# A macaron layer in split fp32: the first two Strassen products of the three output projections change places, and the loads and stores around the middle one move

## The chip, the cores and the metric

The kernel runs on one core of one Trainium2 chip. The metric is the device time of one execution in microseconds (us). Before the change it is 2028.34 us, the median of three runs (2026.97 to 2028.96).

## The reference, cut to what matters

One layer over 1024 tokens of width 1024, all in float32:

```python
h = x + 0.5 * swiglu(rms_norm(h, ffn1_norm), ffn1_w_gate, ffn1_w_up, ffn1_w_down)
z = rms_norm(h, mix_norm) @ w_in             # q, k, v of two attentions, and gates ga, gb
ya = neighbourhood_attention_2d(qa, ka, va, na_rpb)
yb = windowed_gqa_sink(rope(qb), rope(kb), vb, sink_logit)
merged = sigmoid(ga) * (ya @ w_branch_a) + sigmoid(gb) * (yb @ w_branch_b)
h = h + merged @ w_out
h = h + 0.5 * swiglu(rms_norm(h, ffn2_norm), ffn2_w_gate, ffn2_w_up, ffn2_w_down)
return rms_norm(h, final_norm)
```

The hidden width of both feed-forward parts (FFN) is 2816. `swiglu(x, g, u, d)` is `(silu(x @ g) * (x @ u)) @ d`.

## The kernel before

**Split products.** Every float32 operand is split into a high and a low part (`split`, line 87): ScalarE casts the operand to the high part (L88), VectorE or GpSimd subtracts it from the operand and so makes the low part (L89). One product of two blocks is then three matmuls (`mm3`, line 137: L140, L142 and L144) into one PSUM bank.

**Strassen products.** The large products are done with seven block products, P1 to P7, instead of eight. The class `Down` (line 401) runs the second product of each stage, and is used three times: for the down projection of FFN1, for `merged @ w_out` (called the merge here) and for the down projection of FFN2. The left operand has `n` row blocks per half: 11 in the FFNs, 4 in the merge. An entry `(k, p)` is row block `p` of product `k`; it takes 4 column slices `j`, 3 matmuls each, so 12 matmuls of 128x512. The list `ORDER` says in which order the products run: before, P1, P2, P5, P6, P3, P7, P4.

**PSUM banks.** P1, P6, P7 and P4 accumulate in four banks called `g`, P2, P5 and P3 in four banks called `d`. P1, P2 and P5 start new sums, so each needs banks that are free; P6 goes on with P1's sum, P3 with P5's, P7 with P6's and P4 with P7's. After the last entry of P1, P2 and each later product, four VectorE instructions (`evict`, L499) add the sum to the result rows. P5 takes the same four `d` banks as P2, so its first matmul waits until P2's evictions are done. The stage ahead of a `Down` also leaves sums in `g` and `d` banks.

**Preparation.** `prep` (line 448) loads the left operand of an entry from DRAM where there is one (`hid` in the FFNs, `left_d` in the merge, L445), replaces a block of the weights by a difference of two blocks (L458 and L460 on VectorE, L461 and L463 on GpSimd) and splits both operands. It runs `RING` entries ahead of the matmuls (7 in the FFNs, 6 in the merge). `at_end` loads and prepares the first entries of a `Down` while the last products of the hidden stage still run.

**The merge.** Eight chunks of `merged` are computed ahead of it: 24 matmuls each with a weight block of `w_branch_a` (`branch_a`, line 858; loaded in `branch_w`, L839, split with the subtraction on GpSimd), into two banks, `g` and `d` in turn; then VectorE multiplies the two banks by the sigmoid of a gate (L1102, gate loaded at L1073) and adds (L1103). After every second chunk `combine` (line 1080) makes four left operands on GpSimd (L1086) and stores each to `left_d` in DRAM (L1087) from SyncE's queue. The eight loads of `w_out` (L436) stand in the code ahead of the chunk loop.

**What sets the order.** The kernel is written in a tile language. Its scheduler puts the instructions of each engine in an order of its own choosing that keeps the data dependences, from the order in which the code names them. ScalarE, VectorE, GpSimd and SyncE each then run their list in turn; an instruction that waits holds up all that stand behind it on its engine. SyncE's list also issues most DMAs (queue SP in the trace); GpSimd's issues the stores of the hidden stage.

Of the kernel before, what the change touches and what calls it, by code (L numbers as in the profile page):

```python
# [10 lines left out]
F32 = mybir.dt.float32  # L11
# [4 lines left out]
P = 128  # L16
T = 1024
D = 1024
NC8 = D // P
# [12 lines left out]
def f32v(ap):  # L32
    return ap.bitcast(F32)
# [3 lines left out]
def trunk_kernel(ctx, tc, x, n1, wg1, wu1, wd1, nm, win, rpb, sink, wa, wb, wo,  # L37
                 n2, wg2, wu2, wd2, nf, c_rope, c_mask_a, c_mask_b, out):
    nc = tc.nc
# [10 lines left out]
    def nm_(s):  # L50
        uid[0] += 1
        return f"{s}_{uid[0]}"
# [8 lines left out]
    fa = main.tile([P, 4096], F32, name="fa")  # L61
# [6 lines left out]
    def new_ar(g, dt=F32R):  # L68
        ar[g] = main.tile([P, 4, 1024], dt, tag=f"ar{g}", bufs=1, name=nm_("ar"))
        return ar[g]  # L70

    def slot(k):
        return ar[k // 4][:, k % 4, :]

    def bank(tag):
        return ps.tile([P, 512], F32, tag=tag, name=nm_(tag))

    def raw4():
        return main.tile([P, 1024], F32, tag="raw", bufs=4, name=nm_("raw"))

    def xs4():
        return main.tile([P, 1024], F32, tag="xs", bufs=2, name=nm_("xs"))

    def ws4():
        return main.tile([P, 1024], F32R, tag="ws", bufs=8, name=nm_("ws"))

    def split(dst_hi, dst_lo, src, eng=None):
        nc.scalar.copy(dst_hi, src)  # L88
        (eng or nc.vector).tensor_tensor(dst_lo, src, f32v(dst_hi), op=ALU.subtract)  # L89
# [9 lines left out]
    def w_cols(w, c0, n=P):  # L99
        return w[:, c0:c0 + n].rearrange("(c p) f -> p c f", p=P)  # L100
# [45 lines left out]
    def drain(gen, n=1 << 30):  # L146

        for _ in range(n):
            if next(gen, gen) is gen:
                return  # L150

    def res(t):

        return fx[t] if t < 4 else fa[:, (t - 4) * 1024:(t - 3) * 1024]
# [26 lines left out]
    B11, B21, T2, T1, B22, T3, T4 = range(7)  # L181
# [46 lines left out]
    NP = NF // 2  # L228
    PRODUCTS = ("P1", "P2", "P5", "P6", "P7", "P3", "P4")
    RIGHT = dict(P1=B11, P2=B21, P6=T2, P5=T1, P7=T3, P3=B22, P4=T4)  # L230

    def products(src, n, after, at_end, extra, ring, scaled=lambda i, m, half: False):


# [88 lines left out]
        def run():  # L323
            for q in range(len(seq)):
                prep_until(q + 1 if q < 4 else q + 8)
                yield from multiply(q)
                after(*seq[q], bks[seq[q][0]], snap[seq[q][0]], sn)
                at_end(len(seq) - 1 - q)
# [3 lines left out]
    def behind(prods):  # L332
# [9 lines left out]
        return post  # L342

    def hidden(wg, wu, at_end):

        def put(i, p, src):
# [54 lines left out]
    class Down:  # L401

        ORDER = ("P1", "P2", "P5", "P6", "P3", "P7", "P4")

        def __init__(self, n, w, scale, place, left=None, dram=None, loads={}, ring=(22, 24, 26), shift=0):
            self.n, self.w, self.scale, self.place, self.left, self.dram, self.loads = n, w, scale, place, left, dram, loads
            self.seq = [(k, p) for k in self.ORDER for p in range(n)]
            self.dk = [k for k in self.ORDER if k in dram]  # L410
            self.nd = (n + 1) // 2
# [63 lines left out]
        def at_end(self, n):  # L475

            if n == 10:
                self.load_blocks("B11")
            elif n == 7:
                self.load_left(2)  # L480
            elif n in (6, 4, 2, 0):
                if n == 2:
                    self.load_blocks("B21")
                self.prep_until(4 - n // 2)

        def multiply(self, e, j):
# [54 lines left out]

    def down_ffn(wd, src):

        place = {n: [divmod(h0 + p, 8) for p in range(NP)] for n, h0 in (("B11", 0), ("B22", NP), ("B12", NP + 7), ("B21", 2 * NP + 7))}
        place["B22"][7:] = [(f"xs{k // 2}", k % 2) for k in range(4)]
        loads = {}
        for t in range(NTT):
            loads.setdefault(2 + t, []).append(lambda d, t=t: nc.sync.dma_start(res(t), src[t * P:(t + 1) * P, :]))
        for name, e0 in (("B12", 8), ("B22", 19)):
            for a in range((NP + 1) // 2):  # L550
                loads.setdefault(e0 + a, []).append(lambda d, name=name: d.load_blocks(name, 2))
        return Down(NP, wd, 0.5, place, dram={k: hid[i] for i, k in enumerate(PRODUCTS)}, loads=loads)
# [5 lines left out]
    for g in range(7):  # L558
        new_ar(g)
    down = down_ffn(wd1[0], x2)  # L560
    hg = hidden(wg1[0], wu1[0], down.at_end)

# [270 lines left out]
            nc.scalar.copy(gt[:, n * 512:(n + 1) * 512], bs[n])  # L833
        nc.gpsimd.dma_start(g_d[dc * P:(dc + 1) * P, :], gt)

    def branch_w(w, dc, eng=None):

        r, t = raw4()[:, :512], ws4()
        nc.sync.dma_start(r.rearrange("p (c f) -> p c f", f=P), w_cols(w, dc * P))  # L839
        split(t[:, :512], t[:, 512:], r, eng)  # L840
        return [t[:, k:k + 512].rearrange("p (c f) -> p c f", f=P) for k in (0, 512)]

    Y_A, Y_B = ((12, 13), (14, 15), (20, 21), (10, 11)), ((4, 5), (6, 7), (0, 1), (2, 3))

    def branch_mm(bs, w, y):

        for c in range(4):
            mm3(bs, c == 0, c == 3, (w[0][:, c, :], w[1][:, c, :]),
                [[slot(k)[:, n * 512:(n + 1) * 512] for k in y[c]] for n in range(2)])
            yield  # L850
# [2 lines left out]
        load_pair([slot(k) for k in slots], y_d[r0:r0 + P, :], eng)  # L853

    a_order = [dc for p in range(4) for dc in (p, p + 4)]
    a_mm = []

    def branch_a(i):

        w = branch_w(wa[0], a_order[i], nc.gpsimd)  # L860
        bs = [bank("gd"[i % 2]) for _ in range(2)]
        a_mm.append((bs, branch_mm(bs, w, Y_A)))

    def merged(dc):
        return slot((16, 17, 18, 19, 24, 25, 26, 27)[dc])
# [155 lines left out]
    for n in range(1 << 30):  # L1021
# [14 lines left out]
        if n in (59, 60, 61):  # L1036
            c = (59, 60, 61).index(n)
# [7 lines left out]
    drain(fill)  # L1045


    split(slot(10), slot(11), fa[:, 3072:4096])
    for t in range(4):
        new_fx(t)  # L1050

    def load_h(t):
        nc.sync.dma_start(res(t), h_d[t * P:(t + 1) * P, :])


    left_d = dram.tile([4, 4, P, 512], F32, name="left_d")

    def quarter(k, p):
        m = merged(p + (4 if k in ("P2", "P4") else 0))
        return m[:, :512] if k in ("P1", "P2") else m[:, 512:]  # L1060

    place = dict(B11=[(0, p) for p in range(4)], B21=[(0, 4 + p) for p in range(4)],
                 B12=[(1, p) for p in range(4)], B22=[(1, 4 + p) for p in range(4)])
    loads = {t: [lambda d, t=t: load_h(t)] for t in range(NTT)}
    loads[0].append(lambda d: d.load_left(2))
    down = Down(4, wo[0], 1.0, place, quarter, {k: left_d[i] for i, k in enumerate(("P5", "P6", "P3", "P7"))},
                loads, (22, 20), 2)
    for name in ("B11", "B21", "B12", "B22"):
        down.load_blocks(name)

    def a_prep(dc):
        r, rb = raw4(), xs4()
        nc.sync.dma_start(r, g_d[dc * P:(dc + 1) * P, :])  # L1073
        nc.sync.dma_start(rb, g_d[D + dc * P:D + (dc + 1) * P, :])
        nc.scalar.activation(r, r, AF.Sigmoid)
        nc.scalar.activation(rb, rb, AF.Sigmoid)
        nc.vector.tensor_tensor(merged(dc), merged(dc), rb, op=ALU.mult)
        return r

    def combine(p):  # L1080
        a11, a12, a22 = [quarter(k, p) for k in ("P1", "P2", "P4")]
        a21 = merged(p)[:, 512:]
        s = [res(4 + 2 * (p % 2) + k // 2)[:, k % 2 * 512:k % 2 * 512 + 512] for k in range(4)]
        for i, (a, b, op) in enumerate(((a21, a22, ALU.add), (s[0], a11, ALU.subtract), (a12, s[1], ALU.subtract),
                                        (a11, a21, ALU.subtract))):
            nc.gpsimd.tensor_tensor(s[i], a, b, op=op)  # L1086
            nc.sync.dma_start(left_d[i, p], s[i])  # L1087

    nxt = a_prep(a_order[0])
    for i, dc in enumerate(a_order):  # L1090
        r = nxt
        if i + 1 < NC8:
            nxt = a_prep(a_order[i + 1])
        if i + 2 < NC8:
            branch_a(i + 2)
        if i + 1 == NC8:
            down.prep_until(2)
        bs, mm = a_mm[i]
        drain(mm)
        for n in range(2):  # L1100
            sl = slice(n * 512, (n + 1) * 512)
            nc.vector.tensor_tensor(r[:, sl], bs[n], r[:, sl], op=ALU.mult)  # L1102
        nc.vector.tensor_tensor(merged(dc), merged(dc), r, op=ALU.add)  # L1103
        if i % 2:
            combine(i // 2)


    gain = load_gain(n2[0])
    merge = down
    down = down_ffn(wd2[0], h_d)  # L1110
    hg = hidden(wg2[0], wu2[0], down.at_end)

# [75 lines left out]
```

## Time and profile before

| what | value |
|---|---|
| median of three runs | 2028.34 us |
| the profiled execution's own time | 2031.71 us |
| its span, first to last instruction | 2029.9 us |
| TensorE busy | 1952.6 us, 96% |
| VectorE busy | 1437.1 us, 71% |
| ScalarE busy | 963.4 us, 47% |
| GpSimd busy | 414.2 us, 20% |
| mean granted TensorE clock | 0.985 |

The busy share is over the whole span; a stage can differ. The granted clock is 1.00 at TensorE's full speed and 0.50 at half of it. The names in the rows are those of the program: `d<-ws,ws` is an instruction that reads two tiles called ws and writes one called d.

### The profile page before, as it was taken

The page shows a single profiled execution, that of the slowest core. Times are in us where ns is not written, and L with a number is a line of the kernel's source. Part 1 is how long each engine was busy: PE and PEld are TensorE (multiplying, and loading weights), DVE is VectorE, ACT ScalarE, POOL GpSimd, SP SyncE. Part 2 cuts the span into 40 slices and gives each one's busy share as a digit, 9 for nine tenths or more (in the row PEclk, how much of TensorE's full clock was granted, in tenths as well). Part 3 has the DMA queues.
Part 4 walks back from the last instruction along what each step waited for, and adds up shares of the span by engine and source line. Part 5 has one row for each costly group of instructions (what it writes and reads, how often), then busy time and mean ns, then how long its engine had stood idle before and what let it go on. Part 6 is the DMA issues. An engine that isn't in the chain of part 4 may idle for free. (4 is left out here: it accounts for less than half of the span.)

```text
span 2029.9 us, 25701 instructions
## 1 busy us (share of the span) xinstructions
PE 1952.6 (96%) x8968; PEld 1619.9 (80%) x8968; DVE 1437.1 (71%) x2479; ACT 963.4 (47%) x1857; POOL 414.2 (20%) x410
## 2 busy tenths in 40 slices
PE   6999999999999899999999999798999999999998
PEld 5788888888788788788877878586888888887886
DVE  7866566568857777478888855989756656678664
ACT  7433333344346533378887862255333333343453
POOL 4110010004301632111222124404100100114100
PEclk9999999999999999999999999899999999999999
DMA  6423323376234377452334456434332332393341
GB/s 199 135 91 107 115 90 107 114 263 232 90 95 133 120 221 199 135 151 76 104 111 125 163 177 233 151 103 143 118 116 92 104 116 93 117 348 127 103 135 63
DMA packets 224226, 279.83 MB, mean 138 GB/s; under 512 B 13376, under 2 KB 154048, under 8 KB 224096
## 3 DMA queue, kind: packets, MB, share of 16 engines
q1 hardware_dynamic: 204704, 213.58, 33.6%
q0 software_dynamic: 19392, 64.60, 8.9%
q8 instruction: 71, 1.16, 0.2%
q14 instruction: 59, 0.48, 0.1%
HBM read 195.72 MB, written 82.50 MB: 137 GB/s over the span
## 5 line engine op out<-in xcount | busy, mean ns | idle before, releaser
L140 PE MATMUL g<-ar,ws 128*128 128x512 f32 x1208 | 456.2, 399 | 9.6 <-ACT ar L88 4.4
L142 PE MATMUL g<-ar,ws 128*128 128x512 f32 x1208 | 449.1, 393 | 3.7 <-DVE ar L89 3.7
L144 PE MATMUL g<-ar,ws 128*128 128x512 f32 x1208 | 448.3, 393 | 1.8 <-DVE ws L89 1.3
L89 DVE TENSOR_TENSOR ws<-raw,ws 128x512 fp32r<-128x512 f32 (+1 forms) x335 | 254.4, 762 | 202.7 <-ACT ws L88 201.4
L88 ACT CAST ws<-raw 128x512 fp32r<-128x512 f32 (+1 forms) x343 | 217.3, 638 | 318.7 <-PE d L144 124.8
L142 PEld LDWEIGHTS g<-ar,ws 128*128 128x128 f32 x1208 | 228.9, 190 | 52.6 <-DVE ar L89 4.5
L144 PEld LDWEIGHTS g<-ar,ws 128*128 128x128 f32 x1208 | 228.6, 189 | 51.4 <-DVE ws L89 2.1
L140 PEld LDWEIGHTS g<-ar,ws 128*128 128x128 f32 x1208 | 223.4, 190 | 52.3 <-ACT ar L88 6.0
L140 PE MATMUL d<-ar,ws 128*128 128x512 f32 x656 | 255.1, 393 | 7.0 <-DVE ar L89 7.0
L142 PE MATMUL d<-ar,ws 128*128 128x512 f32 x656 | 254.8, 392 | 0.2 <-POOL ar L89 0.2
L144 PE MATMUL d<-ar,ws 128*128 128x512 f32 x656 | 254.4, 392 | 0.1
L347 POOL DMA_DIRECT2D hid<-fx x98 | 52.9, 540 | 498.8 <-DVE fx L374 374.6
L140 PEld LDWEIGHTS d<-ar,ws 128*128 128x128 f32 x656 | 124.4, 190 | 33.7 <-ACT ar L88 4.6
L142 PEld LDWEIGHTS d<-ar,ws 128*128 128x128 f32 x656 | 124.4, 190 | 26.5 <-POOL ar L89 0.6
L144 PEld LDWEIGHTS d<-ar,ws 128*128 128x128 f32 x656 | 124.3, 190 | 26.5 <-POOL ws L89 0.5
L89 DVE TENSOR_TENSOR ws<-ar,ws 128x512 fp32r<-128x512 f32 x110 | 103.7, 948 | 9.1 <-ACT ws L88 7.1
L88 ACT CAST ar<-raw 128x512 fp32r<-128x512 f32 (+1 forms) x83 | 56.0, 678 | 100.0 <-PE g L142 41.4
L89 DVE TENSOR_TENSOR ws<-fa,ws 128x512 fp32r<-128x512 f32 x80 | 55.3, 692 | 63.7 <-ACT ws L88 63.3
L140 PE MATMUL g<-ws,ws 128*128 128x512 f32 x240 | 95.1, 396 | 3.8 <-DVE raw L1102 3.2
L144 PE MATMUL g<-ws,ws 128*128 128x512 f32 x240 | 94.2, 393 | 0.0
L142 PE MATMUL g<-ws,ws 128*128 128x512 f32 x240 | 94.1, 392 | 0.0
L969 ACT ACTIVATE fa<-fa,nmx 128x385 f32<-128x385 f32 (+3 forms) x128 | 75.5, 591 | 28.6 <-DVE nmx L966 27.8
(218 smaller groups left out, 3582.9 us busy)
## 6 DMA issues: line engine op xcount, KB each, us to landing
raw<-hid SPq DMA_DIRECT2D x70, 512.0 KB
hid<-fx POOLq DMA_DIRECT2D x98, 256.0 KB, 2.6
ar<-in_ffn_w_down_dram SPq DMA_DIRECT2D x34, 512.0 KB
raw<-in_ffn_w_up_dram SPq DMA_DIRECT2D x32, 512.0 KB
raw<-in_ffn_w_gate_dram SPq DMA_DIRECT2D x28, 512.0 KB
hid<-fa POOLq DMA_DIRECT2D x56, 256.0 KB, 2.6
raw<-in_w_in_dram SPq DMA_DIRECT2D x27, 512.0 KB
z_d<-fa POOLq DMA_DIRECT2D x36, 256.0 KB, 3.4
```

Of the source, the lines that this page charges most:

```text
L88: nc.scalar.copy(dst_hi, src)
L89: (eng or nc.vector).tensor_tensor(dst_lo, src, f32v(dst_hi), op=ALU.subtract)
L140: nc.tensor.matmul(b, lhs[0], r[0], start=first, stop=False, **kw)
L142: nc.tensor.matmul(b, lhs[0], r[1], start=False, stop=False, **kw)
L144: nc.tensor.matmul(b, lhs[1], r[0], start=False, stop=last, **kw)
L347: nc.gpsimd.dma_start(hid[PRODUCTS.index(p), i], src)
L969: nc.scalar.activation(pr, pr, AF.Exp, scale=-1.0, bias=nmx[:, s:s + 1], accum_out=ssum[:, s:s + 1])
```

## The change

`ORDER` begins with P2, then P1; so P1's entries stand between the last matmul of P2 and the first of P5. To have P2's weights (B21) at hand in the FFNs, `at_end` loads B21 at its third step, ahead of the first `prep`, and `down_ffn` gives B21 and B12 each other's places. In the merge, six of the eight branch weights are loaded into a tile of their own (`fetch_branch`) before the first of `w_branch_b`; the stores of left operands are issued from GpSimd; the loads of `w_out` are named in four parts over the chunks; the gates are prepared two chunks ahead; the last block of `y` and the ring slots move to other tiles.

```diff
-        ORDER = ("P1", "P2", "P5", "P6", "P3", "P7", "P4")
+        ORDER = ("P2", "P1", "P5", "P6", "P3", "P7", "P4")
...
-            elif n in (6, 4, 2, 0):
-                if n == 2:
-                    self.load_blocks("B21")
+            elif n == 6:
+                self.load_blocks("B21")
+            elif n in (4, 2, 0):
                 self.prep_until(4 - n // 2)
...
-        place = {n: [divmod(h0 + p, 8) for p in range(NP)] for n, h0 in (("B11", 0), ("B22", NP), ("B12", NP + 7), ("B21", 2 * NP + 7))}
+        place = {n: [divmod(h0 + p, 8) for p in range(NP)] for n, h0 in (("B11", 0), ("B22", NP), ("B21", NP + 7), ("B12", 2 * NP + 7))}
...
-    def branch_w(w, dc, eng=None):
-
-        r, t = raw4()[:, :512], ws4()
+    def fetch_branch(r, w, dc):
         nc.sync.dma_start(r.rearrange("p (c f) -> p c f", f=P), w_cols(w, dc * P))
+        return r
+
+    def branch_w(w, dc, eng=None, r=None):
+
+        t = ws4()
+        if r is None:
+            r = fetch_branch(raw4()[:, :512], w, dc)
...
-        w = branch_w(wa[0], a_order[i], nc.gpsimd)
+        w = branch_w(wa[0], a_order[i], nc.gpsimd, a_raw.get(i))
...
-    split(slot(10), slot(11), fa[:, 3072:4096])
+    t = new_ar(2, F32)
+    for i in range(2, NC8):
+        a_raw[i] = fetch_branch(t[:, (i - 2) // 2, i % 2 * 512:i % 2 * 512 + 512], wa[0], a_order[i])
+    split(slot(22), slot(23), fa[:, 3072:4096])
...
-                loads, (22, 20), 2)
-    for name in ("B11", "B21", "B12", "B22"):
-        down.load_blocks(name)
+                loads, (8, 10))
...
-            nc.sync.dma_start(left_d[i, p], s[i])
-
-    nxt = a_prep(a_order[0])
+            nc.gpsimd.dma_start(left_d[i, p], s[i])
+
+    nxt = [a_prep(a_order[i]) for i in range(2)]
     for i, dc in enumerate(a_order):
-        r = nxt
-        if i + 1 < NC8:
-            nxt = a_prep(a_order[i + 1])
+        r = nxt.pop(0)
         if i + 2 < NC8:
+            nxt.append(a_prep(a_order[i + 2]))
             branch_a(i + 2)
+        if i % 2 == 0:
+            down.load_blocks(("B21", "B11", "B12", "B22")[i // 2])
+        if i + 3 == NC8:
+            new_ar(2)
```

In the built programs, these are TensorE's first matmuls of the merge's products P1, P2 and P5 (P1 and P2 have four entries of 12 matmuls each; most of them are left out), in the kernel before:

```order
L144 MATMUL d_10748<-ar_4766,ws_10743 128x512
L140 MATMUL g_10867<-ws_10819,ws_10818 128x512
...
L140 MATMUL g_10870<-ar_84 128x512
L142 MATMUL g_10870<-ar_84 128x512
L144 MATMUL g_10870<-ar_84 128x512
L140 MATMUL d_10972<-ws_10887,ws_10886 128x512
...
L140 MATMUL d_11063<-ar_84 128x512
```

and in the changed kernel:

```order
L140 MATMUL d_10864<-ws_10816,ws_10815 128x512
...
L140 MATMUL d_10867<-ws_10882,ws_10881 128x512
L142 MATMUL d_10867<-ws_10882,ws_10881 128x512
L144 MATMUL d_10867<-ws_10882,ws_10881 128x512
L140 MATMUL g_10971<-ar_10750 128x512
...
L140 MATMUL d_11060<-ws_10950,ws_10949 128x512
```

Before, P1 is in g, P2 in d and P5 in d right behind it. Now P2 stands first, in d, then P1 in g, then P5 in d. P2's first entry follows the last chunk, which is in d as well.

This is VectorE's list in the merge from behind P1's evictions to the first of P2's (L499, d) in the kernel before; fx are the result rows, the raw tiles left operands from `left_d`:

```order
L89 TENSOR_TENSOR ar_84<-raw_10872,ar_84 128x512
L89 TENSOR_TENSOR ar_84<-ar_10533,ar_84 128x512
L460 TENSOR_TENSOR ar_10533<-ar_10538,ar_10533 128x512 x2
L89 TENSOR_TENSOR ws_10998<-raw_10874,ws_10998 128x512
L89 TENSOR_TENSOR ws_10999<-ar_10533,ws_10999 128x512
L460 TENSOR_TENSOR ar_10533<-ar_10538,ar_10533 128x512
L89 TENSOR_TENSOR ws_11018<-raw_10874,ws_11018 128x512
L89 TENSOR_TENSOR ws_11019<-ar_10533,ws_11019 128x512
L460 TENSOR_TENSOR ar_10533<-ar_10538,ar_10533 128x512
L89 TENSOR_TENSOR ws_11041<-raw_10876,ws_11041 128x512
L89 TENSOR_TENSOR ws_11042<-ar_10533,ws_11042 128x512
L499 SCALAR_TENSOR_TENSOR fx_10528<-d_10972,fx_10528 128x512
```

and in the changed kernel, from the multiplication of the last chunk (L1111, L1102 before) on:

```order
L1111 TENSOR_TENSOR raw_10738<-d_10749,raw_10738 128x512
L1112 TENSOR_TENSOR ar_10212<-ar_10212,raw_10738 128x1024
L89 TENSOR_TENSOR ws_10881<-ar_10212,ws_10881 128x512
L89 TENSOR_TENSOR ws_10882<-ar_10567,ws_10882 128x512
L89 TENSOR_TENSOR ws_10908<-ar_10211,ws_10908 128x512
L89 TENSOR_TENSOR ws_10909<-ar_10567,ws_10909 128x512
L458 TENSOR_TENSOR ar_10567<-ar_10708,ar_10567 128x512
L89 TENSOR_TENSOR ws_10927<-ar_10211,ws_10927 128x512
...
L89 TENSOR_TENSOR ws_10949<-raw_10869,ws_10949 128x512
L89 TENSOR_TENSOR ws_10950<-ar_10567,ws_10950 128x512
L499 SCALAR_TENSOR_TENSOR fx_10536<-d_10864,fx_10536 128x512
```

Before, P2's evictions (d) stand behind most of P5's and P6's preparation. Now they stand right behind the preparation of P5's first entry, and P1's (g) 12 instructions after those.

This is SyncE's list in the merge before, with g_d the gates:

```order
L436 DMA ar_10533<-in_w_out_dram 128x2x512 x4
L436 DMA ar_10538<-in_w_out_dram 128x2x512 x3
L839 DMA raw_10611<-in_w_branch_a_dram 128x4x128
L1087 DMA left_d<-fa 128x512
L1073 DMA raw_10645<-g_d 128x1024
L1087 DMA left_d<-fa 128x512 x3
L839 DMA raw_10652<-in_w_branch_a_dram 128x4x128
```

and in the changed kernel:

```order
L436 DMA ar_10567<-in_w_out_dram 128x2x512 x4
L436 DMA ar_10708<-in_w_out_dram 128x2x512 x3
L1079 DMA raw_10608<-g_d 128x1024
L1079 DMA raw_10649<-g_d 128x1024
L1079 DMA raw_10696<-g_d 128x1024
L1079 DMA raw_10738<-g_d 128x1024
L445 DMA raw_10869<-left_d 128x2x512
```

The eight loads of `w_out` still stand in one piece. The branch weights and the stores to `left_d` are gone from between the gates.

## Rows read from the trace of the kernel before

**Rows 1.** the head of the page: span, then busy time of each engine

```profile
span 2029.9 us, 25701 instructions
...
PE 1952.6 (96%) x8968; PEld 1619.9 (80%) x8968; DVE 1437.1 (71%) x2479; ACT 963.4 (47%) x1857; POOL 414.2 (20%) x410
```

**Rows 2.** waits of TensorE: total us, times, longest

```profile
PE d L140 <- DVE fx L499: 16.8, 3, 12.1
...
PE g L140 <- DVE raw L1102: 3.2, 1, 3.2
...
PE g L140 <- DVE fx L362: 0.7, 1, 0.7
PE g L144 <- POOL ws L89: 0.4, 1, 0.4
```

**Rows 3.** timeline of TensorE: start, us, instruction, [idle before <-releaser]

```profile
456.35 0.39 PE L140 MATMUL g<-ws,ws 128*128 128x512 f32 x1
...
519.99 0.47 PE L140 MATMUL d<-ws,ws 128*128 128x512 f32 x1 [2.67 <-DVE fx L499]
...
1273.19 0.39 PE L140 MATMUL g<-ws,ws 128*128 128x512 f32 x1
...
1277.86 0.50 PE L140 MATMUL g<-ws,ws 128*128 128x512 f32 x1 [3.15 <-DVE raw L1102]
...
1312.27 0.77 PE L140 MATMUL d<-ar 128*128 128x512 f32 x1 [12.07 <-DVE fx L499]
...
1325.24 0.39 PE L140 MATMUL g<-ws,ws 128*128 128x512 f32 x1
...
1869.31 0.60 PE L140 MATMUL d<-ws,ws 128*128 128x512 f32 x1 [2.02 <-DVE fx L499]
```

**Rows 4.** windows: us, busy by engine, then PEclk, DMA share, GB/s

```profile
521.20:524.70 3.50, 3.50 (x10) 2.69 (x9) 2.84 (x5) 0.26 (x1) 1.12 (x1) 0.51 0.00 0
1272.80:1300.00 27.20, 24.05 (x99) 19.19 (x97) 27.20 (x27) 5.41 (x10) 15.47 (x10) 0.94 0.40 136
1278.90:1282.40 3.50, 3.50 (x10) 2.71 (x9) 3.50 (x5) 2.18 (x4) 2.19 (x2) 0.51 0.71 240
1312.20:1316.50 4.30, 4.23 (x10) 3.39 (x11) 2.92 (x5) 0.00 (x0) 0.00 (x0) 0.50 0.20 70
1869.50:1872.90 3.40, 3.40 (x9) 2.65 (x9) 3.40 (x7) 0.00 (x0) 0.00 (x1) 0.50 0.09 29
```

**Rows 5.** timeline of VectorE around the merge

```profile
1268.53 1.27 DVE L1102 TENSOR_TENSOR raw<-d,raw 128x512 f32<-128x512 f32 x2
...
1271.46 5.74 DVE L89 TENSOR_TENSOR ws<-ar,ws 128x512 fp32r<-128x512 f32 x4
...
1277.13 1.28 DVE L1102 TENSOR_TENSOR raw<-g,raw 128x512 f32<-128x512 f32 x2
...
1311.45 2.47 DVE L499 SCALAR_TENSOR_TENSOR fx<-d,fx 128x512 f32<-128x512 f32 x4
```

**Rows 6.** waits of ScalarE, 1170 to 1312 us

```profile
ACT ws L88 <- DMA raw<-in_w_branch_a_dram: 21.9, 6, 9.6
...
ACT ws L88 <- DMA raw<-left_d: 8.5, 1, 8.5
```

**Rows 7.** windows at the start of FFN1's down projection

```profile
428.00:464.00 36.00, 35.34 (x156) 28.93 (x155) 23.16 (x39) 15.68 (x28) 3.78 (x7) 1.00 1.00 362
468.00:484.00 16.00, 16.00 (x72) 13.27 (x71) 10.98 (x12) 6.86 (x12) 7.29 (x5) 1.00 1.00 373
484.00:517.50 33.50, 33.32 (x148) 27.25 (x146) 33.33 (x38) 13.87 (x25) 18.46 (x12) 1.00 0.37 104
```

**Rows 8.** timeline of VectorE in the same stretch

```profile
453.06 0.68 DVE L369 TENSOR_TENSOR fa<-d,fa 128x512 f32<-128x512 f32 x1
...
481.29 0.69 DVE L458 TENSOR_TENSOR ar<-ar,ar 128x512 f32<-128x512 f32 x1 [4.98 <-DMA ar<-in_ffn_w_down_dram]
```

**Rows 9.** DMA issues on the page: KB each, median us to landing

```profile
hid<-fx POOLq DMA_DIRECT2D x98, 256.0 KB, 2.6
```

More of the change, by code (lines that the diff above doesn't have):

```diff
@@ L834, in gate @@
         nc.gpsimd.dma_start(g_d[dc * P:(dc + 1) * P, :], gt)
-    def branch_w(w, dc, eng=None):
-        r, t = raw4()[:, :512], ws4()
+    def fetch_branch(r, w, dc):
         nc.sync.dma_start(r.rearrange("p (c f) -> p c f", f=P), w_cols(w, dc * P))
+        return r
[3 more added lines that the diff above has]
+            r = fetch_branch(raw4()[:, :512], w, dc)
         split(t[:, :512], t[:, 512:], r, eng)
         return [t[:, k:k + 512].rearrange("p (c f) -> p c f", f=P) for k in (0, 512)]
-    Y_A, Y_B = ((12, 13), (14, 15), (20, 21), (10, 11)), ((4, 5), (6, 7), (0, 1), (2, 3))
+    Y_A, Y_B = ((12, 13), (14, 15), (20, 21), (22, 23)), ((4, 5), (6, 7), (0, 1), (2, 3))
     def branch_mm(bs, w, y):
@@ L855, in trunk_kernel @@
     a_order = [dc for p in range(4) for dc in (p, p + 4)]
-    a_mm = []
+    a_mm, a_raw = [], {}
     def branch_a(i):
-        w = branch_w(wa[0], a_order[i], nc.gpsimd)
+        w = branch_w(wa[0], a_order[i], nc.gpsimd, a_raw.get(i))
         bs = [bank("gd"[i % 2]) for _ in range(2)]
```

## The prediction

> **What bounds the kernel now.** I read the head of the page first: TensorE is busy 1952.6 of 2029.9 us [rows 1], so about 77 us of the span are without a matmul, and only those, and what a low clock costs beside them, can be won. Next I read TensorE's waits by releaser [rows 2]: the largest group is `d L140 <- DVE fx L499`, 16.8 us in three waits, a matmul that starts in a d bank and waits for an eviction. TensorE's timeline puts the three at the start of P5: 2.67 us at 519.99 (FFN1), 12.07 us at 1312.27 (merge), 2.02 us at 1869.31 (FFN2) [rows 3]. That is the wait which `ORDER` decides: P5 takes the banks that P2 has just left. Two smaller waits stand at the start of P1, in g: 3.15 us at 1277.86 in the merge, for the multiplication of chunk 6, and 0.7 us in FFN1 for an eviction of the hidden stage [rows 2, 3].
>
> Then I read the granted clock behind each wait. After the waits that ended at 519.99, 1277.86 and 1869.31 there is a stretch of 3.4 us at 0.50 to 0.51, and after the long one the clock is at 0.50 until 1316.5 [rows 4]; 0.50 is the 1.2 GHz level. At full clock a matmul of 128x512 takes 35.34 / 156 = 0.2265 us [rows 7]. A stretch of 3.4 us at half of it costs 1.7 us. The merge's P5 has 48 matmuls, 10.87 us at full clock, and runs from 1312.27 to 1325.24 [rows 3], 12.97 us, so the low clock costs 2.1 us there.
>
> Last I asked why VectorE is late in the merge. It has no pause from 1272.8 to 1300 [rows 4]. Chunk 6's multiplication starts at 1277.13 [rows 5], 4 us after TensorE has begun P1 (1273.19) and about 9.4 us after chunk 6's own matmuls ended (chunk 7's 24 matmuls, 5.4 us, lie between). Chunk 5's starts at 1268.53, also late, by 6.9 us. Ahead of that ScalarE had waited 21.9 us in six waits for weights of `w_branch_a` [rows 6], whose loads stand in SyncE's list between the stores to `left_d`; the subtractions behind ScalarE's casts then pile up on VectorE (four in 5.74 us at 1271.46 [rows 5]).
>
> **The change part by part.** The count of matmuls stays, so the sum is made of waits.
>
> P5 in the merge. P1's four entries, 48 matmuls or 10.9 us, now lie between P2's last matmul and P5's first. P2's evictions stand in VectorE's list behind the preparation of P5's first entry alone; before, twelve more instructions stood between. The 12.07 us go, and 2.1 us of clock with them: -14.2.
>
> Start of the merge. P2 comes first, in d. Its first two slices take the banks of chunk 5, long free; its third and fourth take chunk 7's, which must be multiplied first, two instructions in 1.27 us as at 1268.53 [rows 5]. Each slice is 3 matmuls, 0.68 us, so the third is due 1.36 us and the fourth 2.04 us after the start. If VectorE is on time this just covers. The 3.15 us and 1.7 us of clock go: -4.85. New is that P2 reads the second halves of `merged`: its fourth entry needs chunk 7, 8.2 us after the start. Multiplication, addition, cast and subtraction are about 1.3 + 1.2 + 0.7 + 0.7 = 3.9 us, and some 7 us if each VectorE step waits for GpSimd: no wait.
>
> Early branch weights. TensorE's wait for a late one is 0.4 us [rows 2]: -0.4. Their true worth is that VectorE comes on time to chunks 5 to 7; the two rows above count on that. `w_out`'s eight loads remain together in SyncE's list: 0 either way, because the four gates behind them are now issued back to back and earlier.
>
> FFN1: the 2.67 us at P5, its 1.7 us of clock, and the 0.66 us at the start of P1 (e = 0 now uses d, whose last hidden sum is read at 453.06 [rows 8], before 456.35 [rows 3]): -5.0. FFN2: 2.02 + 1.7 = -3.7. In both, P1's 11 entries (30 us) now stand between P2 and P5, against a lag of 2 to 2.7 us today. VectorE is busy 33.33 of 33.50 us there [rows 7], but seven entries, 19 us, are prepared ahead; I count nothing for it.
>
> Loading B21 earlier: its first pairs are issued where B12's were, and B21 moves into tiles that come free as early as those did. DMA is saturated in 428 to 464 (share 1.00 [rows 7]). No row shows B21 at this place. From below it costs nothing (it lands ahead of 456.35); from above it lands when the last late weight of this stage does today, 481.29 [rows 8], 25 us late. I take 0, as B12's first pairs, at the same place, held up no matmul.
>
> Stores to `left_d` from GpSimd: 16 issues. GpSimd is busy 15.47 of 27.20 us [rows 4] and has room for them; from the same queue, the hidden stage's stores of 256 KB, the size of these, land in a median of 2.6 us [rows 9]. Below zero they can win at most what ScalarE lost on `left_d`, 8.5 us [rows 6], off TensorE's path once P5 is later; I take 0 and keep the upper end as a rival. The Trainium skill, "SBUF — State Buffer", section "SBUF: two separate sides", speaks against this edit: a DMA from GpSimd's queue has its descriptors written by GpSimd's cores, and those are locked out while VectorE runs an operation in a two-port mode; it advises SyncE's or ScalarE's queue. The 2.6 us were reached beside a VectorE that is busy 71% of the span, so the trace does not bear that rule out as a rule for this kernel; by the rule the sum would be that of the third rival below.
>
> What is late next: P6 takes g behind P1's evictions, at 12 entries x 2.72 = 32.6 us after the start. From chunk 6's multiplication to the end of P2's evictions VectorE took 1277.13 to 1313.92 = 36.8 us today [rows 5]. Its list there has two chunks (two times 1.2 + 1.2), 25 other instructions of 128x512 and eight evictions; four in 2.47 us with 0.68 for one alone is 0.60 each, so 4.8 + 25 x 0.60 + 4.9 = 24.7, and 12.1 us of waiting beside GpSimd. The new list from chunk 7's multiplication to P1's evictions has one chunk, 22 such instructions and eight evictions: 0.3 + 2.4 + 13.2 + 4.9 + 12.1 = 32.9. With less waiting for GpSimd it fits by up to 12 us; with chunk 6 still behind it is 2.4 us later. I take +1.0.
>
> Sum: -14.2 - 4.85 - 0.4 - 5.0 - 3.7 + 1.0 = -27.1. The profiled execution took 2031.71 us, so it would take 2004.6; it lies 3.4 us above the median of 2028.34, which becomes 2001.2.
>
> **The rivals.**
>
> First: VectorE's backlog in the merge stays (the late weights were not its cause). For: four subtractions took 5.74 us beside GpSimd, and the stores add to GpSimd's list. Against: ScalarE's 21.9 us of waits for just these weights. If chunk 6 is again multiplied 4.9 us after the start, chunk 7 follows 1.2 + 1.2 + 1.2 later, at 8.5, and P2's third slice waits 7.1 us, with 1.7 of clock; of the forecast the 4.85 stay to be won, as the old wait is replaced, so 23.3 - 8.8 = 14.5 and 2013.8.
>
> Second: the change doesn't do what it says. `w_out` is not spread, in the built order; if weights stay late too, the 0.4 us remain: 2001.6, inside the forecast's range.
>
> Third: the stores land late. VectorE pauses only when its list has run out, some 21 us after the start; if they land only then, 2.6 us for the store, as much for the load back and 1 for cast and subtraction put P5's first entry at 27.2 in place of 21.8: 5.4 us and 2.1 of clock, 2008.7. Against it: rows 9.
>
> Fourth, on the other side: B21 lands late in both FFNs. P2 as the first product needs it at 456.35, 30 us earlier than today. For: the queues are saturated at that moment. Against: the share of 1.00 ends at 464, and before the change other weights stood there. It is slower than before by over 0.2% (4 us) from the point where each FFN waits 13.9 us (two times 13.9 + 1.7 = 27.1 + 4.1), that is with B21's first pair later than 470. At its full price, 25 + 1.7 in each, 2001.2 + 53.4 = 2054.6; if it lands at 464, 9.4 us in each, 2023.4.
>
> **How the numbers follow.** Forecast 0.60, first rival 0.17, second 0.07, third 0.08, fourth 0.08. 0.2% or 4 us is about what a measurement of this kernel tells from no change. The forecast and the second and third rivals are faster by more; of the first 0.15 is and 0.02 is not; of the fourth 0.07 is slower and 0.01 within. That is faster 0.90, same 0.03, slower 0.07. The forecast's own bounds: with no new wait at P6 and 4 us of smaller waits that go as well, 1996; with P6 late by 3 us and a clock stretch, 2005. The range goes on to the first and third rivals, to 2014, and leaves out the fourth and a little at either end.
>
> **What would show it.** Right: no wait for L499 at the first matmul of P5 in any of the three; no stretch at 0.50 behind those places; the merge's P2 starts without a wait for the chunk's multiplication; ScalarE's waits for `in_w_branch_a` fall to a few us; a small wait, 0 to 3 us, at P6 for L499 in g. Wrong: a wait of 5 us or more in the merge's first entry for the multiplication (first rival), a wait for `left_d` that reaches TensorE at P5 (third), or TensorE waiting in FFN1 or FFN2 for a split of B21 behind a DMA (fourth).

## The result, and the profile after

The changed kernel takes 1997.59 us (median of four runs, 1997.17 to 2001.09), the kernel before 2028.65 us beside it; the ratio is 0.9845, 95% interval 0.9822 to 0.9869. Forecast were 2001.2 us, 27 us less than before; it became 31 us less.

The head of the page of the changed kernel answers to [rows 1]:

```profile
span 1995.4 us, 25679 instructions
...
PE 1939.7 (97%) x8968; PEld 1612.3 (81%) x8968; DVE 1445.2 (72%) x2479; ACT 963.8 (48%) x1857; POOL 420.9 (21%) x426
```

TensorE is busy 12.9 us less for the same count of matmuls, because fewer of them ran at the low clock (the mean granted clock is 0.992, after 0.985), and the span is 34.5 us shorter. The profiled execution before (2031.71 us) was 3.1 us over its median, the one after (1997.17 us) 0.4 us under; so some 31 of the 34.5 us are the change's.

TensorE's waits by releaser in the changed kernel (total us, times, longest), against [rows 2]; the lines of the chunk loop are shifted, L1102 is now L1111:

```profile
...
PE d L140 <- DVE raw L1111: 0.4, 1, 0.4
```

No line for L499 is left, and none for the eviction L362. Of the wait for a chunk's multiplication 0.4 us remain. TensorE's timeline at the places of [rows 3] (P5 in FFN1; P2's first matmul and its third slice, P5 and P6 in the merge; P5 in FFN2):

```profile
515.49 0.39 PE L140 MATMUL d<-ws,ws 128*128 128x512 f32 x1
...
1262.87 0.39 PE L140 MATMUL d<-ws,ws 128*128 128x512 f32 x1
...
1264.80 0.50 PE L140 MATMUL d<-ws,ws 128*128 128x512 f32 x1 [0.41 <-DVE raw L1111]
...
1285.31 0.39 PE L140 MATMUL d<-ws,ws 128*128 128x512 f32 x1
...
1296.19 0.39 PE L140 MATMUL g<-ws,ws 128*128 128x512 f32 x1
...
1835.56 0.39 PE L140 MATMUL d<-ws,ws 128*128 128x512 f32 x1
```

Only the 0.41 us at 1264.80 stand in brackets; P5 starts without a wait in all three. The granted clock behind these places, against [rows 4] (us, busy by engine, then clock, DMA share, GB/s):

```profile
515.00:520.00 5.00, 5.00 (x23) 4.13 (x23) 4.96 (x6) 2.28 (x4) 2.77 (x2) 1.00 0.21 52
1264.50:1269.00 4.50, 4.20 (x19) 3.49 (x20) 3.72 (x5) 2.18 (x4) 3.55 (x5) 1.00 0.93 316
1285.00:1290.00 5.00, 5.00 (x24) 4.14 (x23) 5.00 (x5) 2.38 (x4) 3.70 (x3) 1.00 0.06 24
1835.00:1840.00 5.00, 5.00 (x24) 4.14 (x23) 4.93 (x7) 2.29 (x4) 2.57 (x2) 1.00 0.21 52
```

It is 1.00 in all four, where it was 0.50 or 0.51 before. VectorE in the merge, against [rows 5]:

```profile
1261.35 1.28 DVE L1111 TENSOR_TENSOR raw<-g,raw 128x512 f32<-128x512 f32 x2
...
1264.06 1.27 DVE L1111 TENSOR_TENSOR raw<-d,raw 128x512 f32<-128x512 f32 x2
...
1279.48 2.47 DVE L499 SCALAR_TENSOR_TENSOR fx<-d,fx 128x512 f32<-128x512 f32 x4
...
1293.61 2.47 DVE L499 SCALAR_TENSOR_TENSOR fx<-g,fx 128x512 f32<-128x512 f32 x4
```

Chunk 6 is multiplied at 1261.35, 1.5 us before the merge's P2 begins at 1262.87; before, 4 us after P1 began. P2's evictions end at 1281.95, 3.4 us ahead of P5. P1's run until 1296.08, 0.1 us ahead of P6 at 1296.19. But each slice of P6 needs only the eviction of its own bank, and the first of these four, which took 2.47 us together, began at 1293.61; so the room at P6 was near 2 us, not 0.1. The same holds for P5 before the change: by [rows 3] and [rows 5] it started at 1312.27, while the four evictions ran from 1311.45 to 1313.92. It waited for the first of them, and not, as the part on the PSUM banks has it, until all were done. ScalarE's wait for the branch weights, against [rows 6], and the landing of the stores to `left_d` from GpSimd's queue, against [rows 9]:

```profile
ACT ws L88 <- DMA raw<-in_w_branch_a_dram: 0.3, 1, 0.3
```

```profile
left_d<-fa POOLq DMA_DIRECT2D x16, 256.0 KB, 2.6
```

The 21.9 us have become 0.3. The stores land in a median of 2.6 us.

The table takes the starts of the same products from TensorE's timelines of both profiles and subtracts them; its differences add up to the span's 34.5 us.

| from | to | before, us | after, us | difference | forecast |
|---|---|---|---|---|---|
| start | FFN1's first down product | 456.35 | 455.65 | -0.7 | |
| there | its P6 | 95.30 | 89.76 | -5.5 | -5.0 |
| there | the merge's first product | 721.54 | 717.46 | -4.1 | -0.4 |
| there | its P6 | 52.05 | 33.32 | -18.7 | -18.05 |
| there | FFN2's first down product | 481.85 | 479.53 | -2.3 | |
| there | its P6 | 93.82 | 89.76 | -4.1 | -3.7 |
| there | end | 128.99 | 129.92 | +0.9 | |

The three down projections gave 28.3 us against 26.75 forecast. The rest lies outside them. In the merge's 18.7 us, TensorE's idle time fell by 14.8 us (15.2 to 0.4) and its busy time, at a higher clock, by 3.9 (36.8 to 32.9).

### The profile page after: what moved, and what is told of

Read it like the earlier page. It is cut to its first block, busy times and chain, and to the rows that moved or that the text cites. A ratio compares the mean times of both kernels' runs of the same rounds, so it can differ in the third digit from the quotient of the medians.

```text
span 1995.4 us, 25679 instructions
## 1 busy us (share of the span) xinstructions
PE 1939.7 (97%) x8968; PEld 1612.3 (81%) x8968; DVE 1445.2 (72%) x2479; ACT 963.8 (48%) x1857; POOL 420.9 (21%) x426
## 3 DMA queue, kind: packets, MB, share of 16 engines
q1 hardware_dynamic: 202432, 209.39, 33.2%
## 4 chain that ended last, share of the span: by engine, by line
PE 78%; issue 8%; DVE 6%; POOL 3%; DMA 2%; ACT 2%; SPq 1%; POOLq 0%; DVEq 0%; ACTq 0%
PE g L140 15%; PE g L142 15%; PE g L144 15%; PE d L140 9%; PE d L144 9%; PE d L142 9%; DVE ws L89 2%; PE d L987 1%; POOL z_d L610 1%; PE g L1006 1%; DVE ar L89 1%; DMA raw<-in_w_in_dram 1%; PE d L966 1%; PE d L967 1%; DVE fa L978 1%
## 5 line engine op out<-in xcount | busy, mean ns | idle before, releaser
L88 ACT CAST ws<-raw 128x512 fp32r<-128x512 f32 (+1 forms) x337 | 213.3, 638 | 273.6 <-PE d L144 112.3
L89 DVE TENSOR_TENSOR ws<-ar,ws 128x512 fp32r<-128x512 f32 x114 | 110.5, 976 | 6.6 <-ACT ws L88 6.6
L140 PE MATMUL g<-ws,ws 128*128 128x512 f32 x232 | 91.0, 392 | 0.0
L142 PE MATMUL g<-ws,ws 128*128 128x512 f32 x232 | 90.4, 390 | 0.0
L144 PE MATMUL g<-ws,ws 128*128 128x512 f32 x232 | 90.3, 389 | 0.0
```

What stands on the lines that cost most here:

```text
L140: nc.tensor.matmul(b, lhs[0], r[0], start=first, stop=False, **kw)
L142: nc.tensor.matmul(b, lhs[0], r[1], start=False, stop=False, **kw)
L144: nc.tensor.matmul(b, lhs[1], r[0], start=False, stop=last, **kw)
```

## The experiments

The kernel before was timed beside each set: 2029.3 us beside e2 to e5, 2026.6 beside e7, e8, e10 and e11, 2026.98 beside e12 and e13; so ratios to it are compared across sets.

**The order without the merge's other edits.** `e2_order_ffn` is the kernel before with

```diff
+        ORDER = ("P2", "P1", "P5", "P6", "P3", "P7", "P4")
...
+            elif n == 6:
+                self.load_blocks("B21")
+            elif n in (4, 2, 0):
...
+        place = {... ("B21", NP + 7), ("B12", 2 * NP + 7) ...}
```

Expected: 

> The kernel before with ORDER, the earlier load of B21 and the exchanged places only; the merge's loads and stores stay as they were. Theory (the prediction's steps): FFN1 and FFN2 give back 5.0 + 3.7 us and P5's wait in the merge goes (14.2), but VectorE stays behind with chunks 6 and 7, because the late branch weights stay: the merge's P2 waits some 7 us for the multiplication of the last chunk, with 1.7 us of clock, where P1 waited 3.15 + 1.7. Sum -8.7 - 14.2 + 4 = -19: about 2009 us. Rival A (the order alone is what counts, VectorE's backlog dissolves by itself): no wait of over 1 us at the merge's start, 1998 to 2001 us. Rival B (slower): more than 2028, if P2's need of the last chunk stalls TensorE for over 30 us.

Measured: 2012.77 us, ratio 0.9923 (0.9911 to 0.9936). TensorE's timeline shows a wait for a late weight in a chunk, and the one at P2; the granted clock behind the latter is 0.51, and ScalarE waits 17.1 us for the branch weights:

```profile
1243.57 0.74 PE L144 MATMUL g<-ar,ws 128*128 128x512 f32 x2 [1.34 <-POOL ws L89]
...
1275.40 0.80 PE L140 MATMUL d<-ws,ws 128*128 128x512 f32 x1 [9.03 <-DVE raw L1102]
```

```profile
1275.40:1280.00 4.60, 4.60 (x11) 3.67 (x12) 3.81 (x6) 1.58 (x3) 2.64 (x3) 0.51 0.00 0
```

```profile
ACT ws L88 <- DMA raw<-in_w_branch_a_dram: 17.1, 6, 6.6
```

The theory holds and rival A falls: the new order alone moves 9.0 us of waiting to the merge's start, because P2 needs the banks of chunk 7 at once and VectorE is still behind. The order has removed the wait at P5; what it gains is half of the whole change.

**The merge's edits without the order.** `e5_merge_only` is the changed kernel with

```diff
-        ORDER = ("P2", "P1", "P5", "P6", "P3", "P7", "P4")
+        ORDER = ("P1", "P2", "P5", "P6", "P3", "P7", "P4")
...
+            elif n in (6, 4, 2, 0):
+                if n == 2:
+                    self.load_blocks("B21")
```

and the old places. Expected: 

> The changed kernel with the old ORDER, the old load of B21 and the old places: only the merge's edits. Theory: the FFNs are as before (0). In the merge the wait at P1 goes (4.85) and the wait for a late weight (0.4). P5 still stands right behind P2, so a wait for evictions (L499) stays; VectorE is some 9 us earlier and TensorE 5 us, so the 12.07 us shrink to 7 or 8: in all -10, about 2018 us. Rival A (the whole wait is the order's): P5 waits 12 us or more, 2023 us. Rival B (the whole wait is VectorE's backlog): P5 waits 2.5 us as in the FFNs, 2011 us.

Measured: 2018.43 us, ratio 0.9946 (0.9932 to 0.9959). At the first matmul of P5 TensorE waits 2.43 us in FFN1 and 2.02 us in FFN2. P5 in the merge, and VectorE's evictions of P1 and P2 there:

```profile
1300.87 0.76 PE L140 MATMUL d<-ws,ws 128*128 128x512 f32 x1 [10.41 <-DVE fx L499]
```

```profile
1287.23 2.47 DVE L499 SCALAR_TENSOR_TENSOR fx<-g,fx 128x512 f32<-128x512 f32 x4
...
1300.04 2.47 DVE L499 SCALAR_TENSOR_TENSOR fx<-d,fx 128x512 f32<-128x512 f32 x4
```

The time is the one expected, the wait is not: 10.41 us, nearer to rival A's 12. P1's evictions end at 1289.7, P2's first begins 10.3 us later, behind the preparation of P5 and P6. VectorE came to them 11.4 us earlier than before, but TensorE was done with P2 9.7 us earlier too, so the edits took only 1.7 us off the wait; the rest of the 12.07 us is the order's. The gains of the two halves add up to 16.5 + 10.9 = 27.4 us, the whole change has 31, and 28 in a second measurement (`e13_after_again`); with intervals of 2.5 us either way on each half, it is not shown that they are worth more together.

**Late weights.** `e3_late_weights` is the changed kernel without

```diff
-        a_raw[i] = fetch_branch(t[:, (i - 2) // 2, i % 2 * 512:i % 2 * 512 + 512], wa[0], a_order[i])
```

Expected: 

> The changed kernel, but all branch weights are loaded where they are used, not early. Theory (late weights cause the backlog): ScalarE waits again for in_w_branch_a, over 10 us in all, VectorE comes 3 us or more later to chunks 6 and 7, and the merge's P2 waits 3 to 7 us with a stretch of low clock: 2002 to 2006 us. Rival (it was the stores to left_d in SyncE's list that made the weights late, and these are gone here): no wait of over 1 us, within 0.2% of the changed kernel, 1997 us.

Measured: 2015.05 us, ratio 0.9932 (0.9919 to 0.9944). ScalarE's wait for the weights, and four waits of TensorE, three of them inside the chunks:

```profile
ACT ws L88 <- DMA raw<-in_w_branch_a_dram: 13.1, 6, 4.3
```

```profile
1240.39 0.73 PE L140 MATMUL d<-ar,ws 128*128 128x512 f32 x2 [1.89 <-ACT ws L88]
...
1246.39 1.22 PE L144 MATMUL d<-ar,ws 128*128 128x512 f32 x2 [4.80 <-POOL ws L89]
...
1271.21 0.73 PE L140 MATMUL d<-ar,ws 128*128 128x512 f32 x2 [0.89 <-ACT ws L88]
...
1283.35 0.80 PE L140 MATMUL d<-ws,ws 128*128 128x512 f32 x1 [4.58 <-DVE raw L1111]
```

The direction is the theory's, the size is not: 17 us lost, not 5 to 9. The rival falls, since SyncE's list had no store to `left_d` in it and ScalarE waited 13.1 us for the weights all the same. `e11_late_one_gate` asks whether the gates take the buffers that the weights need:

```diff
-    nxt = [a_prep(a_order[i]) for i in range(2)]
+    nxt = [a_prep(a_order[0])]
...
-            nxt.append(a_prep(a_order[i + 2]))
+        if i + 1 < NC8:
+            nxt.append(a_prep(a_order[i + 1]))
```

(with the late weights). Expected: 

> As the run with late branch weights (2015 us), but the gates are prepared one chunk ahead, as in the kernel before, and not two. Theory (gates two ahead hold the buffers that the late weights need, so the weights waited for a buffer and not for SyncE's list): TensorE's waits within the chunks (1.9, 4.8 and 0.9 us) go, the one at the merge's P2 stays at 4 to 9 us: 2004 to 2009 us. Rival (the weights are late for being loaded where they are used, however many gates are ahead): within 2 us of 2015.

Measured: 2011.01 us, ratio 0.9918 (0.9903 to 0.9934):

```profile
1207.51 0.50 PE L140 MATMUL g<-ar,ws 128*128 128x512 f32 x1 [1.10 <-ACT ar L886]
...
1244.24 1.22 PE L144 MATMUL g<-ar,ws 128*128 128x512 f32 x2 [3.11 <-POOL ws L89]
...
1275.05 0.80 PE L140 MATMUL d<-ws,ws 128*128 128x512 f32 x1 [6.84 <-DVE raw L1112]
```

Neither side is clear: two of the three waits inside the chunks went, one of 3.1 us stays and another of 1.1 us is earlier, and the ratios' intervals overlap. P2 waits 6.84 us. So a gain from fewer gates ahead is not shown; loading the weights early is what counts, by the ratios 15 to 18 us beside the other edits, with the gates one or two chunks ahead. Without it, these other edits gain nothing that can be measured on the order alone (2012.77 us).

**Stores from SyncE's queue.** `e4_stores_sp` is the changed kernel with

```diff
-            nc.gpsimd.dma_start(left_d[i, p], s[i])
+            nc.sync.dma_start(left_d[i, p], s[i])
```

Expected: 

> The changed kernel with the 16 stores to left_d from SyncE's queue again. Theory: two of the four last gate loads stand behind stores that wait for GpSimd, so chunks 6 and 7 may be multiplied a little later; the stores themselves have time on either queue: within 0.2% of the changed kernel, 1997 to 2000 us. Rival A (gates behind the stores make VectorE late): a wait of 3 us or more at the merge's P2, 2002 us or more. [...]

Measured: 1996.70 us, ratio 0.9841 (0.9828 to 0.9855). From 1200 to 1300 us one wait of TensorE is listed:

```profile
PE d L140 <- DVE raw L1111: 0.3, 1, 0.3
```

The queue of the stores decides nothing here: the intervals of both kernels cover each other. The gates behind the stores did not come late enough to matter. The prediction's third rival has no support: the stores from GpSimd's queue landed in 2.6 us, as above, with VectorE busy 34.6 of the 37 us from 1238 to 1275 in which they were issued. The Trainium skill ("SBUF — State Buffer", section "SBUF: two separate sides") says that GpSimd cannot write the descriptors of such DMAs while VectorE runs an operation in a two-port mode. No lateness is seen here, and whether this kernel's VectorE runs such an operation beside the stores, no run shows.

**B21 late.** `e7_b21_late` is the changed kernel with

```diff
-            elif n == 6:
-                self.load_blocks("B21")
-            elif n in (4, 2, 0):
+            elif n in (2, 0):
+                if n == 2:
+                    self.load_blocks("B21")
                 self.prep_until(4 - n // 2)
```

and the old places. Expected: 

> The changed kernel with B21 loaded at the seventh step of at_end, as before, in its old place; P2's first entries are prepared right behind it. Theory (the prediction's fourth rival as a price): B21's first pair lands when DMA is no longer saturated, 5 to 10 us after P2 should begin, and TensorE waits so long in FFN1 and in FFN2, with 1.7 us of clock each: 2011 to 2021 us. Rival A: the load lands ahead of P2, as VectorE and ScalarE are free there: within 0.2% of the changed kernel, 1997 us. Rival B: each later pair is late as well and the entries stall one by one: 2030 us or more.

Measured: 1998.80 us, ratio 0.9853 (0.9835 to 0.9872). P2's first matmul in FFN1 starts with no wait:

```profile
456.63 0.39 PE L140 MATMUL d<-ws,ws 128*128 128x512 f32 x1
```

The theory fell, but not because a late B21 does no harm: it was not late. These are SyncE's issues of B21's first blocks in FFN1, in this run and then in the changed kernel; which blocks they are, the built programs tell:

```profile
435.07 0.88 SPq L436 DMA_DIRECT2D ar<-in_ffn_w_down_dram  x2
```

```profile
439.53 1.39 SPq L436 DMA_DIRECT2D ar<-in_ffn_w_down_dram  x3
```

Named late in the code, the first three of its eleven blocks are issued 4.5 us earlier than in the changed kernel; the other eight follow at 451.4 to 452.9, in place of 434.1 to 440.5, and hold up no matmul. In the kernel before, the first three were already issued at 434.78 and 437.07. So neither this run nor the changed kernel met the condition of the prediction's fourth rival, and what a late B21 would cost was not tested. The moved load and the exchanged places are worth nothing that can be measured.

**GpSimd's price for VectorE.** `e8_sums_dve` is the changed kernel with

```diff
-                nc.gpsimd.tensor_tensor(b12, b22, b12, op=ALU.subtract)
+                (nc.vector if self.n == 4 else nc.gpsimd).tensor_tensor(b12, b22, b12, op=ALU.subtract)
```

and the same for b21. Expected: 

> The changed kernel with the eight weight differences L461 and L463 of the merge on VectorE instead of GpSimd. In the changed kernel P1's evictions end 0.1 us before P6 starts. Theory (a VectorE instruction of two operands beside a GpSimd one waits 1.1 us, and one more on VectorE takes 0.6): four or five of the eight stand ahead of P1's evictions, so these end 2 to 3 us earlier against P6's start; TensorE has no wait there to lose, so the time is within 0.2% of the changed kernel, 1997 us. Rival (GpSimd costs VectorE nothing): the evictions end 2.4 to 3 us later, P6 waits, 2000 us or more.

Measured: 1996.63 us, ratio 0.9846 (0.9828 to 0.9863). P1's evictions on VectorE:

```profile
1288.14 2.47 DVE L499 SCALAR_TENSOR_TENSOR fx<-g,fx 128x512 f32<-128x512 f32 x4
```

The evictions end at 1290.61, 5.1 us ahead of P6 (1295.69), where the changed kernel had 0.1. More than expected, since six GpSimd instructions went from that stretch and VectorE got only three of them ahead of the evictions: 6 x 1.1 - 3 x 0.6 = 4.8. The time is the same, as TensorE had no wait there.

**The room at P6.** `e10_split_twice` adds to the changed kernel

```diff
+            if self.n == 4 and k == "P5":
+                split(t[:, :512], t[:, 512:], b11)
```

Expected: 

> The changed kernel in which the right operand of the merge's four P5 entries is split twice: four more casts on ScalarE, four more subtractions on VectorE ahead of P1's evictions. Theory (P1's evictions have 0.1 us of room before P6): P6 waits 2.3 us, up to 4.5 if the four stand beside GpSimd's work, with up to 1.7 us of clock: 1999.5 to 2003.5 us. Rival (there is room, VectorE's order adapts): no wait for L499 at P6, 1997 us.

Measured: 1999.20 us, ratio 0.9863 (0.9845 to 0.9882). VectorE's evictions of P1, the last of the differences for P6 (L460), and TensorE at P2's third slice and at P6:

```profile
1292.74 2.47 DVE L501 SCALAR_TENSOR_TENSOR fx<-g,fx 128x512 f32<-128x512 f32 x4
...
1298.64 0.68 DVE L460 TENSOR_TENSOR ar<-ar,ar 128x512 f32<-128x512 f32 x1
```

```profile
1266.64 0.50 PE L140 MATMUL d<-ws,ws 128*128 128x512 f32 x1 [1.64 <-DVE raw L1113]
...
1298.07 0.39 PE L140 MATMUL g<-ws,ws 128*128 128x512 f32 x1
```

The theory fell: P6 starts without a wait, P1's evictions end 2.9 us before it. The 0.1 us was no edge, since P6 needs only the first of the four evictions, and since the work in front of them can move. The scheduler put one difference (L460) behind them that stood ahead before. More came from GpSimd, whose differences (L463) cost VectorE nothing here ahead of the evictions. The first of them, and VectorE beside it:

```profile
1288.13 5.85 POOL L463 TENSOR_TENSOR ar<-ar 128x512 f32<-128x512 f32 x1 [7.29 <-DVE ar L460]
```

```profile
1289.73 1.28 DVE L460 TENSOR_TENSOR ar<-ar,ar 128x512 f32<-128x512 f32 x2
```

VectorE goes on at 0.6 us for each instruction, and the span of GpSimd's is 5.85 us in place of 1.6 to 1.7.

**Both together, beside the changed kernel itself.** `e12_sums_dve_sp` has the differences on VectorE in all three down projections and the stores in SyncE's queue; `e13_after_again` is the changed kernel.

```diff
-                nc.gpsimd.tensor_tensor(b12, b22, b12, op=ALU.subtract)
+                (nc.vector).tensor_tensor(b12, b22, b12, op=ALU.subtract)
...
-            nc.gpsimd.dma_start(left_d[i, p], s[i])
+            nc.sync.dma_start(left_d[i, p], s[i])
```

Expected: 

> The changed kernel with all weight differences L461 and L463 on VectorE, in the FFNs too, and the stores to left_d in SyncE's queue. Theory: VectorE gains 0.5 us for each moved instruction, but TensorE has no wait left that ends on them, in none of the three down projections; so no gain beyond 0.1%: 1995 to 1998 us, within 0.2% of the changed kernel run beside it. Rival: what VectorE saves also shortens the waits in the transition after the merge (2.8, 1.9 and 0.7 us) or the stretches of low clock: 3 us or more faster than the changed kernel.

And: 

> The changed kernel itself, as the measure for the run beside it: 1996 to 1999 us.

Measured: 1994.30 us (1993.99 to 1999.99), ratio 0.9846 (0.9827 to 0.9865), against 1998.68 us (1996.41 to 1999.73), ratio 0.9860 (0.9843 to 0.9876). The intervals overlap, and no difference is shown. P2's third slice in the second:

```profile
1267.37 0.50 PE L140 MATMUL d<-ws,ws 128*128 128x512 f32 x1 [1.39 <-DVE raw L1111]
```

In the profiled execution of the first the 2.8 us wait of the transition is still there, so on this wait the rival falls. But that execution took 1999.99 us, and three of the five 1994; so a gain of 3 us or more by the clock, the other half of the rival, is neither shown nor ruled out. The second shows how far one profile of the same kernel differs from another: the wait that was 0.41 us is 1.39 here.

## Why the prediction was right

**P5 behind P1** (-14.2). Right. The 12.07 us and the low clock are gone. That the order does it, and not only an earlier VectorE, is shown by the merge's edits without it, where 10.4 us of the wait stay, and by the order alone, which leaves no wait for L499.

**The merge's start** (-4.85). Right in size: 0.4 us remain in one profile, 1.4 in another. The condition that VectorE is on time proved the hinge. Without the early weights P2 waits 4.6 to 9.0 us at this place, and the time is 2011.0 to 2015.1 us, where the first rival had put 2013.8. That it came so near is in part luck: its sum leaves out the 4.85 us although it says that the old wait is replaced, and with them it is 2009; two of the three runs lost 3 to 8 us more to late weights inside the chunks, which it did not have.

**Early weights** (-0.4). The term was booked in the wrong place more than wrong. It had only TensorE's own wait for a weight, and a sentence that the other two terms count on it. Measured beside the rest, the early weights are worth 15 to 18 us, about as much as the order gains alone (16.5). Gates two chunks ahead may add to it; that is not settled.

**FFN1 and FFN2** (-5.0, -3.7). Right: -5.5 and -4.1 by the table.

**B21 and the stores to `left_d`** (0 and 0). Right: the stores' queue made no difference, and B21 made no wait. For B21 the room that I gave it was not what was tested: its first blocks are issued 16 us ahead of P2 in the changed kernel and 22 us in the run that names them late, in FFN1 and FFN2 alike. In the fourth rival I also misread [rows 7]: the DMA share is 1.00 from 468 to 484 too and does not end at 464; and the price for a landing at 464 counts the clock twice, it is 2020.0 and not 2023.4.

**P6** (+1.0). Wrong, the wait did not come. The estimate of VectorE's work was close, 32.9 us against 33.2 measured from P2's start to the end of P1's evictions. But the term counted to the end of all four, and P6 needs only the first, which is done some 1.8 us earlier: 31.1 by the estimate, ahead of P6 at 32.6 as I had set it and at 33.3 as it came.

**What was left out.** About 4 us. One of them is P6's. Another part lies in the transition behind the merge, 2.3 us by the table. TensorE there in the changed kernel, and in `e2_order_ffn`, which has the old merge edits:

```profile
1361.27 0.47 PE L140 MATMUL g<-ar,ws 128*128 128x512 f32 x1 [2.81 <-DVE fa L369]
...
1379.49 0.47 PE L140 MATMUL d<-ar,ws 128*128 128x512 f32 x1 [1.85 <-DVE ar L89]
```

```profile
1372.94 0.47 PE L140 MATMUL g<-ar,ws 128*128 128x512 f32 x1 [2.00 <-DVE fa L369]
...
1393.71 0.77 PE L140 MATMUL d<-ar,ws 128*128 128x512 f32 x1 [4.20 <-DVE ar L89]
```

The wait of 4.2 us is 1.85 with the merge's edits (1.9 to 2.0 in `e3_late_weights` and `e5_merge_only`) and stays without them, while the wait ahead of it grows from 2.0 to 2.8. So both belong to these edits, and not to the order; which of them, the ring slots or the moved tiles, was not separated. The 4.1 us between FFN1 and the merge are another matter, taken up at the end.

## What to carry to other kernels

Where two products use the same banks in turn, putting one that uses other banks between them hides the eviction; but the first product of the new order takes over the wait for whatever held its banks, so make the engine that frees those be on time first. An engine that waits for a DMA only in passing can set the time two steps later: TensorE's own wait for a late weight was 0.4 us before the change, and the early weights are worth 15 to 18 us beside the new order. A load that stands later in the code need not be issued later, so an experiment on a late load shows something only where the trace shows it late.

## What the runs showed of the hardware

VectorE and GpSimd hold each other up. Two subtractions of VectorE in the changed kernel, the second beside GpSimd's difference that follows them in the rows:

```profile
1291.30 0.69 DVE L89 TENSOR_TENSOR ws<-raw,ws 128x512 fp32r<-128x512 f32 x1
...
1291.90 1.78 DVE L89 TENSOR_TENSOR ws<-ar,ws 128x512 fp32r<-128x512 f32 x1
```

```profile
1291.52 1.61 POOL L463 TENSOR_TENSOR ar<-ar 128x512 f32<-128x512 f32 x1 [1.42 <-DVE ar L460]
```

The first, begun before GpSimd's, takes 0.69 us, the second 1.78. Taking six such GpSimd instructions away brought 5.0 us on VectorE, although three more ran on it there. It is not always VectorE that pays: in `e10_split_twice`, above, it ran on undisturbed and the span of GpSimd's difference grew to 5.85 us.

The low clock is not a fixed price of a wait. In the kernel before a wait of 2.27 us was followed by a stretch of low clock; the same wait, 2.30 us, in `e2_order_ffn` was not. The two waits, and the granted clock behind each, the kernel before first:

```profile
1183.45 0.77 PE L140 MATMUL g<-ar,ws 128*128 128x512 f32 x1 [2.27 <-ACT xs L833]
```

```profile
1183.40:1186.90 3.50, 3.45 (x8) 2.79 (x9) 3.45 (x4) 1.34 (x3) 2.78 (x2) 0.51 0.28 114
```

```profile
1174.88 0.70 PE L140 MATMUL g<-ar,ws 128*128 128x512 f32 x2 [2.30 <-ACT xs L833]
```

```profile
1174.80:1178.30 3.50, 3.42 (x15) 2.90 (x16) 3.47 (x3) 1.38 (x3) 2.84 (x2) 1.00 0.23 95
```

The granted clock is 0.51 in the first and 1.00 in the second, which got through almost twice the matmuls in the same time. This is what the table shows between FFN1's P6 and the merge, in the kernel before and in the changed one:

```profile
551.65:1273.19 721.54, 700.94 (x3490) 590.82 (x3488) 520.53 (x1155) 429.96 (x912) 179.95 (x144) 0.99 0.47 146
```

```profile
545.41:1262.87 717.46, 696.78 (x3490) 588.01 (x3489) 538.40 (x1172) 430.02 (x912) 192.22 (x158) 0.99 0.48 148
```

TensorE is idle for 20.6 us in one and 20.7 in the other. All of the 4.1 us is busy time for the same matmuls, that is clock, and in `e13_after_again`, the changed kernel once more, the busy time of this stretch is 699.2 us. So a difference of this kind arises between executions of one kernel too, and should not be credited to the change.
